# Other charges in the planner that merges TensorE's threads, in a float32 kernel of three transformer layers

## The chip, the core and the metric

The kernel runs on one core of a Trainium2 chip. The metric is the device time of one execution in microseconds, as the median over runs. The profile shows five engines and their queues: TensorE (PE, with its weight loads as PEld), VectorE (DVE), ScalarE (ACT), GpSimd (POOL) and SyncE (SP), which issues the loads of the weights.

## What is computed

A sequence of 256 tokens with 1024 features, with 16 meta tokens ahead of it (272 rows, T = 272), goes through two blocks in float32. The first block has a layer with a gated delta rule and a convolutional feed-forward, and a layer with an mLSTM and the same feed-forward. The second block has a gated feed-forward, three branches side by side (spatial gating, latent attention, attention over a memory of 256 rows) that gates merge, and another gated feed-forward. Cut to its core:

```python
hs = hs + rms_norm(gated_deltanet(rms_norm(hs)))   # 16 heads of 128, chunks, triangular solve per chunk
hs = hs + rms_norm(conv_ffn(rms_norm(hs)))         # 1024 -> 2 x 2816 -> 1024, 3-tap convolution
hs = hs + rms_norm(mlstm(rms_norm(hs)))            # 4 heads
hs = hs + rms_norm(conv_ffn(rms_norm(hs)))
x  = x + 0.5 * swiglu(rmsnorm(x))                  # second block
h  = rmsnorm(x); z = h @ w_in
merged = (gate_a * (spatial_gating(z) @ w_a) + gate_b * (mla(z) @ w_b)
          + gate_c * (memory_attention(z, mem) @ w_c))
x  = x + merged @ w_out
x  = x + 0.5 * swiglu(rmsnorm(x))
```

## The kernel before

Every product of the float32 layers is split into a high and a low part, and three passes (high by high, high by low, low by high) are added up in PSUM. A weight tile comes by a DMA from SyncE's queue (`wraw`), ScalarE makes its high part (`wh`), and VectorE or GpSimd the low part (`wl`). `linear_g` runs such a product: for each tile of weights of 256 columns it issues 48 matmuls for two output tiles of 128 rows.

The order on TensorE is neither written out by hand nor left to the framework. The program is written as Python generators ("threads"). One main thread holds the large products. In some stages side threads are added: in the gated delta rule four lanes that invert the triangular matrices (`wy_inverse`, `gdn_core`), two threads that prepare keys and queries (`before`, with `unit_kq` and `gdn_pre`), one that gates the outputs; in the mLSTM one thread per head; in the branches one each for rope, latent norms, spatial gating and attention. A thread yields a list of tiles that its next matmuls need, at times with an extra delay in us. `Threads.run` keeps a clock for TensorE: it resumes the first thread in its list whose tiles are ready by that clock, and the thread that is ready earliest if none is. Side threads stand ahead of the main thread, so that the large products fill in only where no side thread is ready.

When a tile is ready is what the planner works out while the program is being built. `note` sees each instruction that a thread issues. On TensorE it adds a cost to the clock. On another engine it looks for the first gap in that engine's planned time after its inputs are ready (`place`), as long as the instruction's cost: a fixed part plus one per column, from the table `COST`, times a factor `KC`. `ready` adds a lag when a tile is read: `PLAG` from TensorE to another engine and for a PSUM bank to come free, `LAG` between two other engines, `SAME` on one engine. Casts of weights are placed from TensorE's clock on and count as ready.

`first` sets `KC` and the three lags anew ahead of the gated delta rule, after it, and ahead of the branches. The class's own values hold only until the first of these.

Only TensorE's instructions are pinned to the merged order. The queues of the other engines are ordered by the tile framework, which starts from the order in which the program issues them; some stretches on VectorE and ScalarE are in program order by hand. The thread `projections` chooses between the next group of projections and one of the z products by whether the lanes' preparation of two groups before is over in the plan.

Every recorded instruction stands on line 190, in the engine's wrapper, or on line 383, so the rows are told apart by tiles: `ps` is the output of a large product, `yp`, `w`, `zp` and `r2p` are the products of the inverse, `RT` its two matrices, `Y` a copy between them, `kqp` the transposed keys and queries, `kqtok` their scaled copy, `otp` the transposed outputs, `on` the outputs, `rq_a`, `rq_y` and `rq_o` the steps of a Newton chain for a reciprocal square root (11 instructions, `rsqrt_small`), `cy` the steps of the four-tap filter (three on VectorE for each tile), `zth` the first copy of a z product.

Of the kernel before, what the change touches and what calls it, by code (L numbers as in the profile page):

```python
# [96 lines left out]
class Threads:  # L97
# [1 line left out]

    LAG, SAME, PLAG = 0.25, 0.13, 0.6
    KC = 1.0
    COST = {"PE": (0.0, 1 / 2400), "A": (0.06, 0.00085), "V": (0.07, 0.00104), "G": (0.1, 0.0022)}

    def __init__(self):
        self.clk = {"PE": 0.0}
        self.busy = {k: [] for k in self.COST}
        self.rdy, self.read, self.bank = {}, {}, {}
# [24 lines left out]
    def note(self, key, outs, ins, n, ahead=False):  # L134
        a, b = self.COST[key]
        t = max([self.ready(x, key) for x in ins], default=0.0)
        if key == "PE":
            t = self.clk["PE"] = max(t, self.clk["PE"]) + a + b * n
        else:
            t = self.place(key, self.clk["PE"] if ahead else t, (a + b * n) * self.KC)  # L140
        for x in ins:
            self.read[x.tensor.name] = max(t, self.read.get(x.tensor.name, 0.0))
        for o in outs:
            self.rdy[o.tensor.name] = (0.0, key) if ahead else (t, key)
# [64 lines left out]
class Kern:  # L209
# [1496 lines left out]
    def first(self):  # L1706

        i = self.i
        X = self.embed()
        self.th.KC, self.th.LAG, self.th.SAME, self.th.PLAG = 0.8, 0.25, 0.18, 0.65  # L1710
        Y = yield from self.gdn(X)
        self.th.KC, self.th.LAG, self.th.SAME, self.th.PLAG = 0.9, 0.25, 0.13, 0.6
        self.ordered = True
        self.gctx.close()
        self.pb = self.pool(self.ctx, "pb", 1, space=PSUM)
        self.pp = self.pool(self.ctx, "pp", 3, space=PSUM)
        self.p_v = self.pool(self.ctx, "pkv", 8)
        self.p_m = self.pool(self.ctx, "pm", 1)
        self.p_s2 = self.pool(self.ctx, "psm2", 2)
        b1 = ExitStack()  # L1720
        self.p_b1 = self.pool(b1, "pb1", 1)
        self.p_c = self.pool(b1, "pcore", 12)
        self.lane = None
        vectors = self.vectors_b()
        self.th.add([self.sumsq(self.half, vectors)])
        self.mix_begin(self.hs, T)
        yield from self.project_out(i["gdn_w_out"][0], Y, 16, T, lambda m, p: self.mix_tile(m, p, 8, T))
        X = yield from self.mix_end(self.hs, 16, T, self.ffn_loads(i["ffn_w_up"][0]))
        Y = yield from self.conv_ffn(X, 0, T, 0)
        self.mix_begin(self.hs, T)  # L1730
        yield from self.project_out(i["ffn_w_down"][0], Y, KF, T, lambda m, p: self.mix_tile(m, p, 24, T))
        W = i["ml_w_in"][0]
        X = yield from self.mix_end(self.hs, 32, T, [
            (W, 0, KD, 3072, 8, lambda name, dt: self.cst((128, KD, 8), dt, name, f"m{name}")),
            (W, 0, 4, 0, 256), (W, 0, 4, 512, 256), (W, 4, 4, 0, 256)])
        self.ordered = False
        self.mixing = False
        Y = yield from self.mlstm(X, S + 2)
        self.ordered = True
        self.th.add([self.mem_rows()])  # L1740
        N = S + 2
        hs = [h[:, T - N:] for h in self.hs]
        self.mix_begin(hs, N)

        def then():
            yield from self.ml_heads
            self.mem_load(0, 1)

        yield from self.project_out(i["ml_w_out"][0], Y, 8, N, lambda m, p: self.mix_tile(m, p, 40, N), then)
        self.pause[0].set()  # L1750
        X = yield from self.mix_end(hs, 48, N, self.ffn_loads(i["ffn_w_up"][1]))
        Y = yield from self.conv_ffn(X, 1, N, 2)
        hs = [h[:, NM:] for h in self.hs]
        self.mix_begin(hs, S)
        yield from self.project_out(i["ffn_w_down"][1], Y, KF, S, lambda m, p: self.mix_tile(m, p, 56, S))
        self.pause[1].set()
        X = yield from self.mix_end(hs, PV_F1, S, self.ffn_loads(i["ffn1_w_gu_2"][0]), full=False)
        self.x2 = hs

        def extra(c):  # L1760
            if c == 1:
                self.rope_tables()
                self.th.add([self.mem_keys()])
                self.mem_load(4, 5)
            elif c == 4:
                yield from self.mem_product(4, 5)
            elif c == 7:
                self.mem_load(6, 7)
            elif c == 9:
                yield from self.mem_product(6, 7)  # L1770
                self.mem_done.set()

        Y = yield from self.swiglu_up(X, i["ffn1_w_gu_2"][0], extra, True)
        self.add_begin(PV_MIX)
        yield from self.project_out(i["ffn1_w_down_2"][0], Y, KF, S, lambda m, p: self.add_tile(m, p, 0.5))
        X = self.nextX
        yield self.mem_done
        b1.close()
        self.p_c = None
        self.p_b2 = self.pool(self.ctx, "pb2", 1)  # L1780
        self.th.KC, self.th.LAG, self.th.SAME, self.th.PLAG = 0.9, 0.3, 0.13, 0.7
        yield from self.mixers(X)
        yield from self.last()

# [663 lines left out]
```

## Time and profile before

| | before |
|---|---|
| median of 3 runs | 1668.43 us (1667.3 to 1671.02) |
| the profiled execution | 1671.11 us, span of its instructions 1669.3 us |
| TensorE / VectorE / ScalarE / GpSimd busy | 94% / 67% / 56% / 35% |
| mean granted clock of TensorE | 0.973 |

The span is the time from the first to the last recorded instruction. Busy shares are means over stages with different limits, so each stage is read by itself. In all views times are us unless marked ns; a wait names the instruction that waited and, behind the arrow, the one whose end released it.

### The profile page before, as it was taken

How to read it: one execution, taken by the hardware profiler on the slowest of the kernel's cores; microseconds unless marked ns; L12 is line 12 of the kernel's file. 1: busy time of each engine (PE TensorE's matmuls, PEld its weight loads, DVE VectorE, ACT ScalarE, POOL GpSimd, SP SyncE). 2: the span in 40 equal slices, each digit the busy share in tenths (PEclk: the TensorE clock that was granted, in tenths of full speed). 3: DMA queues.
4: the chain of work that ended last, by engine and by line, in shares of the span. 5: the costliest groups of instructions: out<-in, count | busy, mean ns of one | idle time of the engine just before them, and what ended most of it. 6: DMA issues, size and time to landing. Idle time of an engine off the chain costs nothing.

```text
span 1669.3 us, 31255 instructions
## 1 busy us (share of the span) xinstructions
PE 1564.4 (94%) x11980; PEld 1475.4 (88%) x11980; DVE 1120.0 (67%) x2223; ACT 927.9 (56%) x1877; POOL 579.2 (35%) x535
## 2 busy tenths in 40 slices
PE   8889888899999998999899998999997899999999
PEld 6788778799899997888899998999985789999987
DVE  5788877766888757457877668464659663566643
ACT  4567767655566554446566556454553655564542
POOL 3574555320200002550344441122275548511221
PEclk9799999999999999999999999999998999999999
DMA  5331221226355554335366564566553335656564
GB/s 158 89 89 52 69 64 47 77 90 214 106 178 174 169 175 111 96 115 164 107 185 192 175 185 148 163 199 192 173 166 111 111 93 150 183 164 188 180 189 151
DMA packets 239100, 235.39 MB, mean 141 GB/s; under 512 B 11511, under 2 KB 226407, under 8 KB 238951
## 3 DMA queue, kind: packets, MB, share of 16 engines
q1 hardware_dynamic: 238326, 231.86, 46.4%
q8 instruction: 94, 1.54, 0.4%
q0 software_dynamic: 496, 1.41, 0.4%
q14 instruction: 56, 0.45, 0.1%
q10 hardware_dynamic: 128, 0.13, 0.0%
HBM read 232.32 MB, written 1.05 MB: 140 GB/s over the span
## 4 chain that ended last, share of the span: by engine, by line
PE 68%; DVE 22%; ACT 5%; DMA 3%; issue 2%; POOL 0%; ACTq 0%; POOLq 0%; DVEq 0%
PE ps L190 52%; PE pst L190 5%; DVE cy L190 3%; DVE rq_a L190 3%; ACT wh L190 2%; DVE RT L190 2%; DVE wl L190 1%; DVE rq_y L190 1%; PE memp L190 1%; DMA wraw<-in_ffn_w_up_dram 1%; DVE xn L190 1%; PE rsp L190 1%; DVE on L190 1%; PE w L190 1%; PE up L190 1%
## 5 line engine op out<-in xcount | busy, mean ns | idle before, releaser
L190 PE MATMUL ps<-xhl,wh 128*128 128x256 f32 (+2 forms) x4496 | 861.6, 294 | 28.9 <-DVE py L190 11.1
L190 PEld LDWEIGHTS ps<-xhl,wh 128*128 128x128 f32 x4496 | 703.0, 193 | 38.3 <-DVE py L190 6.9
L190 ACT CAST wh<-wraw 128x1024 fp32r<-128x1024 f32 (+2 forms) x436 | 448.0, 1029 | 389.8 <-PE ps L190 255.9
L190 PE MATMUL ps<-xhl,wl 128*128 128x256 f32 (+2 forms) x2248 | 626.0, 287 | 0.8 <-DVE wl L190 0.8
L383 POOL TENSOR_TENSOR wl<-wraw,wh 128x512 fp32r<-128x512 f32 (+3 forms) x264 | 334.7, 1291 | 658.2 <-ACT wh L190 622.8
L190 PEld LDWEIGHTS ps<-xhl,wl 128*128 128x128 f32 x2248 | 423.9, 192 | 1.0 <-DVE wl L190 1.0
L190 DVE TENSOR_TENSOR wl<-wraw,wh 128x1024 fp32r<-128x1024 f32 (+2 forms) x237 | 287.4, 1213 | 182.4 <-ACT wh L190 179.2
L190 POOL TENSOR_TENSOR wl<-wraw,wh 128x512 fp32r<-128x512 f32 x134 | 173.9, 1319 | 153.1 <-ACT wh L190 136.2
L190 PE MATMUL ps<-hh,wh 128*128 128x256 f32 (+1 forms) x1056 | 191.1, 283 | 0.0
L190 PEld LDWEIGHTS ps<-hh,wh 128*128 128x128 f32 x1056 | 163.2, 189 | 0.0
L190 PE MATMUL ps<-hh,wl 128*128 128x256 f32 (+1 forms) x528 | 149.7, 284 | 0.0
L190 DVE SCALAR_TENSOR_TENSOR fy<-ps,pvt,fy 128x256 f32<-128x256 f32 (+2 forms) x176 | 84.9, 488 | 25.1 <-ACT fy L190 23.2
L190 PEld LDWEIGHTS ps<-hh,wl 128*128 128x128 f32 x528 | 99.4, 188 | 0.0
L190 DVE SCALAR_TENSOR_TENSOR cy<-cx,pvt,cy 128x271 f32<-128x271 f32 (+2 forms) x96 | 74.5, 779 | 13.5 <-ACT cy L190 12.5
L190 DVE TENSOR_TENSOR hh<-fy,hh 128x256 fp32r<-128x256 f32 (+1 forms) x88 | 64.4, 735 | 13.2 <-ACT hh L190 12.8
L190 POOL MEMSET mvt<- 128x4 f32 x4 | 0.4, 102 | 176.0 <-PE ps L190 176.0
L190 ACT ACTIVATE fy<-ps,pvt 128x272 f32<-128x272 f32 (+1 forms) x88 | 49.5, 568 | 12.3 <-PE ps L190 11.8
L190 DVE TENSOR_TENSOR py<-ps,rstd 128x256 f32<-128x256 f32 x72 | 29.9, 420 | 37.9 <-PE ps L190 37.9
L190 PE MATMUL pst<-wh,hh 128*128 128x512 f32 x176 | 55.1, 394 | 0.0
L190 ACT CAST hh<-fy 128x256 fp32r<-128x256 f32 (+1 forms) x88 | 35.7, 407 | 29.8 <-DVE fy L190 29.0
L190 DVE CAST_PREDICATED RT<-lvl,w 128x512 f16<-128x512 uint8 x67 | 44.9, 683 | 7.1 <-PE w L190 6.8
L190 PE MATMUL ps<-og,wh 128*128 128x272 f32 x256 | 48.6, 289 | 0.1
(523 smaller groups left out, 2420.4 us busy)
## 6 DMA issues: line engine op xcount, KB each, us to landing
wraw<-in_ffn_w_up_dram SPq DMA_DIRECT2D x88, 512.0 KB
wraw<-in_ffn_w_gu_dram SPq DMA_DIRECT2D x88, 512.0 KB
wraw<-in_ffn_w_down_dram SPq DMA_DIRECT2D x79, 512.0 KB
wraw<-in_gdn_w_in_dram SPq DMA_DIRECT2D x48, 512.0 KB
wraw<-in_w_in_dram SPq DMA_DIRECT2D x41, 512.0 KB
wraw<-in_ml_w_in_dram SPq DMA_DIRECT2D x24, 512.0 KB
wraw<-in_gdn_w_out_dram SPq DMA_DIRECT2D x16, 512.0 KB
wraw<-in_ml_w_out_dram SPq DMA_DIRECT2D x8, 512.0 KB
```

Of the source, the lines that this page charges most:

```text
L190: r = f(*args, **kw)
L383: eng.tensor_tensor(l[:, a, b], r[:, a, b], h[:, a, b].bitcast(F32), ALU.subtract)
```

## The change

The table of charges gets other numbers: a fixed part for TensorE, larger fixed parts for ScalarE and VectorE, a larger one per column for GpSimd and TensorE. The factor `KC` goes, and so do the three places where `first` sets it and the lags. One set of lags is left for all stages; `SAME` is 0.05.

```diff
-    LAG, SAME, PLAG = 0.25, 0.13, 0.6
-    KC = 1.0
-    COST = {"PE": (0.0, 1 / 2400), "A": (0.06, 0.00085), "V": (0.07, 0.00104), "G": (0.1, 0.0022)}
+    LAG, SAME, PLAG = 0.25, 0.05, 0.6
+    COST = {"PE": (0.006, 0.000441), "A": (0.19, 0.00084), "V": (0.155, 0.00104), "G": (0.1, 0.0025)}
...
         if key == "PE":
             t = self.clk["PE"] = max(t, self.clk["PE"]) + a + b * n
         else:
-            t = self.place(key, self.clk["PE"] if ahead else t, (a + b * n) * self.KC)
+            t = self.place(key, self.clk["PE"] if ahead else t, a + b * n)
...
         X = self.embed()
-        self.th.KC, self.th.LAG, self.th.SAME, self.th.PLAG = 0.8, 0.25, 0.18, 0.65
         Y = yield from self.gdn(X)
-        self.th.KC, self.th.LAG, self.th.SAME, self.th.PLAG = 0.9, 0.25, 0.13, 0.6
         self.ordered = True
...
         self.p_b2 = self.pool(self.ctx, "pb2", 1)
-        self.th.KC, self.th.LAG, self.th.SAME, self.th.PLAG = 0.9, 0.3, 0.13, 0.7
         yield from self.mixers(X)
```

## Rows read from the trace of the kernel before

**Rows 1.** The page: span, and busy us (share of the span) of each engine

```profile
span 1669.3 us, 31255 instructions
...
PE 1564.4 (94%) x11980; PEld 1475.4 (88%) x11980; DVE 1120.0 (67%) x2223; ACT 927.9 (56%) x1877; POOL 579.2 (35%) x535
```

**Rows 2.** Windows: stretch, length, busy us of each engine (instructions), granted clock, DMA

```profile
core 0: us, PE busy (x) PEld busy (x) DVE busy (x) ACT busy (x) POOL busy (x), PEclk, DMA share, GB/s
50.00:350.00 300.00, 260.04 (x2175) 236.84 (x2175) 242.43 (x571) 201.83 (x620) 167.77 (x185) 0.95 0.25 71
640.00:800.00 160.00, 147.08 (x1041) 130.45 (x1039) 100.03 (x245) 81.45 (x178) 55.01 (x46) 0.98 0.39 113
1210.00:1400.00 190.00, 170.01 (x1208) 155.32 (x1207) 125.44 (x359) 99.53 (x214) 109.01 (x89) 0.96 0.42 121
550.00:600.00 50.00, 50.00 (x401) 50.00 (x401) 31.17 (x45) 25.61 (x39) 0.00 (x0) 1.00 0.55 170
```

**Rows 3.** TensorE's waits, 50 to 350 us: total us, times, longest us

```profile
PE yp L190 <- DVE RT L190: 13.7, 10, 3.3
PE kqp L190 <- ACT kqtok L190: 6.7, 4, 3.5
PE otp L190 <- DVE on L190: 5.0, 3, 4.4
PE zp L190 <- DVE RT L190: 4.8, 5, 2.2
```

**Rows 4.** TensorE's waits, 1210 to 1400 us

```profile
PE ps L190 <- DVE py L190: 6.3, 1, 6.3
PE sgy L190 <- DVE sgyy L190: 4.0, 1, 4.0
PE ptp L190 <- ACT pexp L190: 2.9, 1, 2.9
```

**Rows 5.** TensorE's longest wait, 640 to 800 us

```profile
PE mbp L190 <- DVE mlf L190: 4.3, 1, 4.3
```

**Rows 6.** VectorE's groups by shape, 50 to 350 us: busy us, mean ns, idle before

```profile
L190 DVE CAST_PREDICATED RT<-lvl,w 128x512 f16<-128x512 uint8 x67 | 44.9, 683 | 7.1 <-PE w L190 6.8
...
L190 DVE TENSOR_TENSOR rq_a<-rq_a,rq_v 128x4 f32<-128x4 f32 x24 | 8.0, 344 | 0.3
...
L190 DVE MEMSET mga<- 128x24 f32 x1 | 0.1, 78 | 0.0
```

**Rows 7.** ScalarE's groups by shape, 50 to 350 us

```profile
L190 ACT CAST wh<-wraw 128x1024 fp32r<-128x1024 f32 x41 | 43.0, 1049 | 8.2 <-POOL wl L190 3.9 <-issue 2.1 <-PE ps L190 1.1
...
L190 ACT ACTIVATE tcb<-tcb 128x2 f32<-128x2 f32 x1 | 0.2, 197 | 0.0
```

**Rows 8.** One tile over the whole run: duration ns min/median/max, first and last start

```profile
L190 DVE TENSOR_TENSOR rq_a<-rq_a,rq_v x99: 143/161/1277, 9.4 to 1351.8; 128x4 f32<-128x4 f32 x57, 128x3 f32<-128x3 f32 x15, 128x8 f32<-128x8 f32 x15, 128x2 f32<-128x2 f32 x6
```

**Rows 9.** Timelines of VectorE and GpSimd, 194.7 to 198 us: start, us, what

```profile
194.80 0.16 DVE L190 SCALAR_TENSOR_TENSOR rq_a<-rq_y 128x4 f32<-128x4 f32 x1
...
195.34 1.21 DVE L190 TENSOR_TENSOR rq_a<-rq_a,rq_v 128x4 f32<-128x4 f32 x1
196.58 1.19 DVE L190 SCALAR_TENSOR_TENSOR rq_y<-rq_a,rq_y 128x4 f32<-128x4 f32 x1
...
195.25 2.50 POOL L190 TENSOR_TENSOR wl<-wraw,wh 128x512 fp32r<-128x512 f32 x2 [0.66 <-ACT wh L190]
```

**Rows 10.** Windows of the products' tile alone (its PE column is their busy time)

```profile
330.00:340.00 10.00, 6.55 (x44) 5.76 (x44) 0.86 (x2) 0.79 (x2) 1.00 0.19 52
340.00:350.00 10.00, 7.29 (x47) 6.20 (x45) 0.43 (x1) 0.79 (x2) 0.91 0.36 108
```

**Rows 11.** The z products' first copies: ns min/median/max, first and last start

```profile
L190 ACT ACTIVATE zth<-ps x16: 372/397/431, 266.5 to 372.5; 128x272 f32<-128x272 f32 x16
```

## The prediction, made before the changed kernel ran

> **What bounds the kernel now.** I read the totals first, then TensorE's waits, then the engines that it waits for. TensorE is busy for 94% of the span [rows 1]; between the stages that mix threads its products run back to back, 401 matmuls of 272 columns in 50 us, 0.125 us each, with no idle time [rows 2]. Nothing there can move, since one thread alone issues. The change can act where the merge has several threads to choose from: the gated delta rule (50 to 350 us), the mLSTM (640 to 800) and the branches (1210 to 1400). TensorE's idle time there is 40.0, 12.9 and 20.0 us [rows 2], 73 us in all, and that is the pool from which any gain comes. What a reader should see in the waits [rows 3 to 5]: TensorE stands at a lane's instruction, put into its order too early, while VectorE or ScalarE still makes its operand. In the first stage the lanes' inverse (yp and zp, waiting for RT) takes 18.5 us in 15 waits; the transposes behind a Newton chain (kqp and otp) take 11.7 us in 7. In that stage VectorE is busy for 242 of 300 us [rows 2]: close to a bound of its own, so not all of the 40 us can be won.
>
> **The change, part by part.** Nothing is added to or taken from the chip's work. The constants are used while the program is built; the same matmuls, copies and DMAs are issued, in another order on TensorE. The queues of the other engines and SP's loads follow the program's order, so they move with it. Instruction costs are therefore zero on each engine, and the sum consists of waits alone.
>
> What the merge compares is a delay with a number of products put ahead of it, so I convert both sets into products of 272 columns. A product is charged 272/2400 = 0.1133 us before and 0.006 + 272 x 0.000441 = 0.1260 us after; the chip takes 0.125 us [rows 2]. So every delay counts in units that are 11% larger.
>
> *A hop without a queue.* From a matmul through one RT merge (512 columns on VectorE) back to TensorE: before 0.65 + 0.8 x (0.07 + 512 x 0.00104) + 0.25 = 1.382 us, 12.2 products; after 0.6 + 0.155 + 0.532 + 0.25 = 1.537 us, 12.2 products. Through one ScalarE copy of 256 columns: before 0.65 + 0.8 x (0.06 + 0.218) + 0.25 = 1.122 us, 9.9 products; after 0.6 + 0.19 + 0.215 + 0.25 = 1.255 us, 10.0 products. No difference: the shorter lags cancel the longer instructions. So the change does nothing to a lane that meets no queue.
>
> *The queue.* Here the sets differ. VectorE's 49 groups in this stage hold 571 instructions with 109,864 columns (the first and the last of them, and one between, in [rows 6]). Before they are charged 0.8 x (571 x 0.07 + 109,864 x 0.00104) = 123 us, or 1089 products; after 571 x 0.155 + 114.3 = 203 us, or 1610 products; the engine is busy for 242 us. One RT merge is charged 0.48 us before, 0.69 after, and takes 0.683 [rows 6]. ScalarE's 554 instructions with 149,972 columns, in 32 groups without the 66 reads of an accumulator, which are not charged (first and last in [rows 7]), go from 129 to 231 us, against 202 busy [rows 2]. So the plan after sees a queue on VectorE where the plan before saw an engine half idle, and sends a lane's matmul later, with products in front of it.
>
> How much later? Four lanes do the inverse side by side, so up to three RT merges stand in front of one: each is charged 0.69 against 0.48/0.9 = 0.54 in the same units, 0.15 us more, 0.46 for three. Three filter steps (271 columns) in front instead: 0.437 against 0.313, 0.37 for three. I take 0.4 us a wait, in the middle. Fifteen waits x 0.4 = 6.0 us gained, of 18.5 [rows 3]. The bounds: nothing, if the products put ahead were needed later to cover another wait; the whole 18.5 us at most.
>
> *Newton chains.* Eleven tiny VectorE instructions, each after the one before: before 0.18 + 0.8 x 0.074 = 0.239 us each, 23.2 products for the chain; after 0.05 + 0.159 = 0.209 us, 18.3 products. So, without a queue, kqp and otp come 4.9 products, 0.62 us, too early. With a queue at 0.4 us per wait the two nearly cancel: I take zero for the 7 waits (11.7 us now), bounds -2.8 and +8.1 us (13 such chains, 9 before kqp and 4 before otp, x 0.62).
>
> *The other two stages.* In the mLSTM a hop of 256 columns on VectorE is 0.6 + 0.9 x 0.336 + 0.25 = 1.153 us, 10.8 products of 256 (0.1067), and after 1.271 us, 10.7 (0.1189): nothing; its longest wait, 4.3 us, is a chain of tiny instructions with no products beside it that the merge sets [rows 5]. In the branches the lags were longer: 0.7 + 0.303 + 0.3 = 1.303 us, 12.2 products, against 10.7. There the plan after sends lanes 1.5 products, 0.18 us, earlier. The 6.3 us wait for py is a PSUM buffer that products wait for, which no thread's readiness shows [rows 4]; it stays. The other waits are few; I charge +1 us, bounds -4 and +4.
>
> Sum: -6 + 0 + 1 = -5 us. The profiled execution took 1671.1 us (span 1669.3, 1.8 around it), so 1666.1; it lies 2.7 above the median of the runs, 1668.4, and for a run like the median I forecast 1663 us, 0.3% less.
>
> **A rule that speaks against the charges.** The four-element instruction behind "rq_a" takes 143 ns at the least, 161 in the median and 1277 at the most [rows 8]. The timeline shows one such at 0.16 us, and then two at 1.21 and 1.19 us while GpSimd runs two subtractions of 512 columns [rows 9]. The Trainium skill, page SBUF — State Buffer, section "SBUF: two separate sides", says that VectorE with two SBUF inputs (or in a two-port mode) and GpSimd take their common port pair as an exclusive lock for a whole instruction. The trace agrees: the held instruction lasts about as long as GpSimd's. By that rule no fixed part plus columns gives VectorE's time, in either set, and the gain would be near nothing.
>
> **Rivals.** *No change to be told* (within 0.2%, 3.3 us, which is about what a measurement of this kernel tells from no change): TensorE waits because VectorE was held by GpSimd, not because a charge was short. For it: a held instruction costs 1.0 us more than its charge, more than the 0.4 that the change adds to a queue; and VectorE's busy 242 us stay above the 203 charged. Against it: RT itself takes 0.683 on average and is charged exactly that. Result 1665 to 1672.
>
> *Slower by the chains.* A mechanism of its own: the lag between two instructions of one engine falls from 0.18 to 0.05 us, and with it goes a slack that covered the held instructions. It decides if the queue adds less than 0.62 us to a Newton chain in the plan. For it: the means of rq_a are 344 ns [rows 6] against 209 charged. Price: up to 13 x 0.62 = 8 us, and no gain at RT: 1676.
>
> *Slower by an early end of the products.* ScalarE is charged 231 us where it is busy for 202, so the plan's lanes fall behind the chip's, and products run ahead. The last z products cover the lanes' end: 6.6 + 7.3 us of products between 330 and 350 us [rows 10]. If they are used up before, the lanes' last hops stand bare: +10 to +14 us, 1680. The first z tile comes at 266 us today, after all projections [rows 11]; the projections' thread puts a z product in front of a projection whenever the lanes' preparation is late in the plan, which is where this would begin. Against it: 8 z products of 48 matmuls are a long reserve.
>
> *Much faster.* If the orders fit so well that half of the stage's 40 us goes: 1648.
>
> **How the numbers follow.** The forecast's mechanism, more products ahead of lanes that queue at VectorE: 0.45, 0.10 of it the large gain. No difference to be told: 0.25. Slower by the chains: 0.17. Slower by early products: 0.13. Faster 0.45, same 0.25, slower 0.30. The time is that of the likeliest, 1663; its own range is 1652 to 1665. The range takes in the other cases down to the large gain and up to the early end, 1649 to 1679, and leaves out their tails, about 2 in 10.
>
> **What would show it.** Right: the same instruction counts; the waits of yp and zp for RT in the first stage fall from 18.5 us to about 12, TensorE's idle time there from 40 to about 34 us, and VectorE's busy time stays near 242. The chains: kqp and otp above 11.7 us. The early end: z tiles before 266 us, or TensorE idle between 330 and 360. Wrong altogether: the first stage as long as before with its idle time only moved, or a difference that comes from a stage with one thread, by another order of loads or of GpSimd's share.

## The result, and the profile after

The changed kernel takes 1717.28 us (median of four runs, 1715.38 to 1717.59); the kernel before, measured beside it, 1667.87 us. The ratio is 1.0284, with a 95% interval of 1.0265 to 1.0303: slower by 2.8%, where 0.3% faster was forecast. The page of the changed kernel, its totals and the clock that TensorE was granted in 40 equal slices:

```profile
span 1715.6 us, 31253 instructions
PE 1587.4 (93%) x11980; PEld 1495.2 (87%) x11980; DVE 1116.1 (65%) x2223; ACT 931.1 (54%) x1877; POOL 579.8 (34%) x535
PEclk9899989987999999999999999999999999999999
```

Every engine issues as many instructions as before [rows 1], and VectorE, ScalarE and GpSimd are busy as long within 4 us: only the order changed. But the clock's digits show an 8 and a 7 in the ninth and tenth slice, 343 to 429 us, where the page of the kernel before has nines. So I cut the run where stages hand over, at the first matmul of a product that opens the next one, and for `mm` at its last (us):

| from, to | before | after | more |
|---|---|---|---|
| start, the gated delta rule's output product (`og`) | 368.3 | 403.0 | 34.7 |
| `og`, the mLSTM's gates (`psmg`) | 275.6 | 279.1 | 3.5 |
| `psmg`, the branches' first product (`krp`) | 572.3 | 575.8 | 3.5 |
| `krp`, the branches' last product (`mm`) | 258.6 | 263.0 | 4.4 |
| `mm`, end | 194.5 | 194.7 | 0.2 |

Three quarters of the 46.3 us are lost in the first stage that mixes threads. Windows of that stage, cut at 300 us and at its end, for the kernel before (columns as in [rows 2]):

```profile
50.00:300.00 250.00, 215.78 (x1791) 195.74 (x1790) 204.85 (x470) 171.59 (x532) 145.37 (x166) 0.94 0.25 71
300.00:368.30 68.30, 61.88 (x524) 58.05 (x523) 42.91 (x117) 40.15 (x110) 24.93 (x21) 0.98 0.26 78
```

and after:

```profile
50.00:300.00 250.00, 218.75 (x1760) 204.29 (x1759) 181.68 (x391) 159.75 (x450) 161.37 (x173) 0.92 0.32 91
300.00:403.00 103.00, 72.24 (x539) 59.93 (x538) 64.04 (x201) 56.15 (x191) 7.28 (x14) 0.83 0.04 11
```

Length minus TensorE's busy time is its idle time. Up to 300 us it is 31.3 us after against 34.2 before, 3 us better. From there to the end it is 30.8 against 6.4, 24.4 us worse, and the same work takes longer: TensorE is busy for 291.0 us over both windows against 277.7, 13.3 more, at a granted clock of 0.83 in the last window where it was 0.98. These three, -3.0 + 24.4 + 13.3, are the 34.7 us. The 13.3 us are not the clock's alone: one matmul of the product `og` lasts 288 ns in the median, but back to back one follows every 125 ns [rows 2], so a matmul that stands alone counts for more busy time than one in a row; no run separates the two. The other columns say what is missing at the end: VectorE did 391 instructions up to 300 us where it had done 470, and the DMA share of the last window is 0.04 where it was 0.26: there are no weights left to load, so no products left to run.

TensorE's waits after, 50 to 400 us, so that the longer stage is taken in whole (total, times, longest):

```profile
PE yp L189 <- DVE RT L189: 13.6, 9, 3.8
PE ps L189 <- ACT cy L189: 8.9, 6, 5.2
PE ps L189 <- DVE zs L189: 8.7, 4, 6.4
PE kqp L189 <- ACT kqtok L189: 6.3, 4, 2.1
PE otp L189 <- DVE on L189: 4.6, 3, 2.2
...
PE zp L189 <- DVE RT L189: 0.8, 2, 0.5
```

In the same window the rows of the kernel before are those of [rows 3], and its products wait for their buffers for 3.8 us:

```profile
PE ps L190 <- DVE zs L190: 2.6, 3, 1.9
...
PE ps L190 <- ACT cy L190: 1.2, 2, 1.0
```

The inverse waits 14.4 us for RT against 18.5, the Newton chains 10.9 us against 11.7. (Up to 350 us alone, the window of [rows 3], it is 12.3 and 7.0 us, but by then the changed kernel has not done as much of the stage.) The waits that the change could shorten did get shorter, by 4.9 us; against that, products wait 17.6 us for the buffers that VectorE (`zs`) and ScalarE (`cy`) read out, 13.8 more. What else it paid shows where products are. The z products' first copies (ns at least, in the median, at most; first and last start):

```profile
L189 ACT ACTIVATE zth<-ps x16: 391/401/478, 116.3 to 305.2; 128x272 f32<-128x272 f32 x16
```

The first comes at 116 us, not at 266, and the last at 305 instead of 372 [rows 11]. The windows of the products' tile alone (`ps`), from the start until the fourth lane has finished its inverse, before:

```profile
0.00:151.84 151.84, 79.29 (x463) 67.49 (x463) 0.00 (x0) 14.00 (x36) 0.89 0.35 100
```

and after, with three stretches of the stage's end:

```profile
0.00:193.16 193.16, 123.78 (x768) 109.36 (x768) 3.04 (x7) 21.64 (x55) 0.91 0.41 114
...
300.00:310.00 10.00, 3.48 (x21) 2.61 (x20) 0.86 (x2) 0.81 (x2) 0.95 0.32 103
310.00:320.00 10.00, 0.00 (x0) 0.00 (x0) 0.00 (x0) 0.00 (x0) 0.71 0.01 3
...
390.00:400.00 10.00, 0.00 (x0) 0.00 (x0) 0.00 (x0) 0.00 (x0) 0.50 0.00 0
```

The stage has 1152 such matmuls. After, 768 of them have run when the first four lanes are through, before 463. The 305 more take 38 us at 0.125 us each [rows 2], and the first group is 41.3 us late. From then on the four groups of lanes follow each other as before: from the end of the first group's inverses to that of the fourth 180.0 us against 177.5. What is left of the stage then takes 29.8 us against 39.0; together 41.3 + 2.6 - 9.2 = 34.7 us. The last product has run at 310 us, 93 us before the stage ends, where before products filled the stretch up to its end [rows 10]. In that bare stretch the granted clock goes up and down: 1.00 from 320 to 340 us, 0.83 from 340 to 370, and 0.50, the lower of its two levels, 1.2 GHz, from 390 to 400. One kind of matmul of the lanes' last steps, before:

```profile
L190 PE MATMUL up<-wq,St x32: 195/276/276, 352.9 to 356.2; 128*128 128x32 f32 x32
```

and after:

```profile
L189 PE MATMUL up<-wq,St x32: 261/401/401, 387.7 to 394.2; 128*128 128x32 f32 x32
```

276 ns became 401. The Trainium skill, page TensorE: Matmul & The Clock Gate, section "Part 1: The HAM clock gate", has a half-rate state that activity lifts; the trace agrees, with the granted 0.50 and the 401 ns above, and with 1.00 from 410 to 420 us, when products run back to back again.

### The profile page after: what moved, and what is told of

It reads as the page before. It is cut to its first block, busy times and chain, and to the rows that moved or that the text cites. A ratio compares the mean times of both kernels' runs of the same rounds, so it can differ in the third digit from the quotient of the medians.

```text
span 1715.6 us, 31253 instructions
## 1 busy us (share of the span) xinstructions
PE 1587.4 (93%) x11980; PEld 1495.2 (87%) x11980; DVE 1116.1 (65%) x2223; ACT 931.1 (54%) x1877; POOL 579.8 (34%) x535
## 4 chain that ended last, share of the span: by engine, by line
PE 72%; DVE 17%; ACT 6%; DMA 2%; issue 2%; POOL 1%; ACTq 0%; POOLq 0%; DVEq 0%
PE ps L189 55%; PE pst L189 4%; DVE cy L189 2%; DVE rq_a L189 2%; ACT wh L189 2%; DVE RT L189 1%; PE memp L189 1%; DVE rq_y L189 1%; DVE wl L189 1%; PE warm L189 1%; PE up L189 1%; PE rsp L189 1%; PE w L189 1%; DVE xhl L189 1%; PE dp L189 1%
## 5 line engine op out<-in xcount | busy, mean ns | idle before, releaser
L189 PE MATMUL ps<-xhl,wh 128*128 128x256 f32 (+2 forms) x4496 | 864.2, 295 | 44.3 <-DVE py L189 10.6
L189 PEld LDWEIGHTS ps<-xhl,wh 128*128 128x128 f32 x4496 | 710.7, 194 | 54.9 <-ACT cy L189 10.5
L189 PEld LDWEIGHTS ps<-xhl,wl 128*128 128x128 f32 x2248 | 428.2, 194 | 0.9 <-DVE wl L189 0.9
L189 DVE SCALAR_TENSOR_TENSOR cy<-cx,pvt,cy 128x271 f32<-128x271 f32 (+2 forms) x96 | 74.8, 783 | 14.3 <-ACT cy L189 11.7
L189 DVE TENSOR_TENSOR hh<-fy,hh 128x256 fp32r<-128x256 f32 (+1 forms) x88 | 60.6, 691 | 13.4 <-ACT hh L189 13.2
L189 ACT ACTIVATE fy<-ps,pvt 128x272 f32<-128x272 f32 (+1 forms) x88 | 49.6, 569 | 13.8 <-PE ps L189 13.2
L189 DVE CAST_PREDICATED RT<-lvl,w 128x512 f16<-128x512 uint8 x67 | 45.1, 683 | 11.7 <-PE w L189 11.3
```

The lines of the kernel that those rows point to most:

```text
L189: r = f(*args, **kw)
```

## The experiments

The theory after the result: larger charges put the lanes' instructions later in the plan, products go ahead of the first group's chain, and they are missing at the end. Its rivals: the loss is in the other stages; it comes from the one place where z products are chosen; from GpSimd, which held the products' copies; or the lanes simply meet longer waits. A last question was whether an order between the two does better. This table is worked out from the windows of each run like those above: ratio to the kernel before, products run until the fourth lane's inverse and the time of that, end of the stage, TensorE's idle time from 50 to 300 us and from 300 us to the stage's end.

| kernel | ratio | products | 4th lane, us | stage's end, us | idle to 300 | idle after 300 |
|---|---|---|---|---|---|---|
| before | 1 | 463 | 151.8 | 368.3 | 34.2 | 6.4 |
| e11 tie order | 1.0052 | 464 | 153.9 | 374.4 | 37.1 | 6.1 |
| e1 old set in the stage | 1.0148 | 464 | 154.0 | 379.1 | 35.7 | 12.2 |
| f1 new lags only | 1.0152 | 447 | 151.2 | 386.3 | 42.5 | 12.5 |
| e5 charges x 0.6 | 1.0220 | 414 | 141.6 | 393.5 | 45.8 | 17.2 |
| e12 PSUM seen | 1.0169 | 450 | 154.1 | 391.8 | 44.2 | 14.0 |
| g2 longer lag | 1.0174 | 483 | 153.0 | 391.2 | 39.8 | 14.6 |
| f3 dearer products | 1.0138 | 493 | 153.6 | 382.2 | 39.7 | 11.1 |
| e3 old ScalarE charge | 1.0196 | 525 | 162.6 | 389.3 | 37.0 | 16.2 |
| f2 shorter occupancy | 1.0213 | 549 | 168.8 | 395.1 | 37.7 | 17.7 |
| e6 charges x 0.8 | 1.0179 | 552 | 167.0 | 383.2 | 43.7 | 12.9 |
| g1 x 0.8, old lags | 1.0189 | 561 | 165.0 | 385.7 | 33.6 | 17.2 |
| e4 z last | 1.0242 | 576 | 168.9 | 392.4 | 34.0 | 20.9 |
| e7 old VectorE charge | 1.0396 | 694 | 198.0 | 422.2 | 42.8 | 28.8 |
| e8 no GpSimd filter | 1.0217 | 729 | 173.7 | 391.1 | 27.9 | 27.5 |
| e2 new set in the stage | 1.0242 | 741 | 197.7 | 405.0 | 33.5 | 26.9 |
| after | 1.0284 | 768 | 193.2 | 403.0 | 31.3 | 30.8 |

e9 and e10 (below) leave this stage as it was before. Their profiles end it at 365.2 and 364.2 us, with 34.0 and 37.9 us idle up to 300 us and 6.3 and 6.4 behind it, so a difference of about 4 us between two rows tells nothing. Diffs that set the table or the lags for this stage set them back behind it; a short diff shows the changed part of the table or of the lags only.

**Which stage.** The kernel before with the new set in the gated delta rule alone, and the changed kernel with the old one there:

```diff
-        self.th.KC, self.th.LAG, self.th.SAME, self.th.PLAG = 0.8, 0.25, 0.18, 0.65
...
+        self.th.COST, (self.th.LAG, self.th.SAME, self.th.PLAG) = {"PE": (0.006, 0.000441), "A": (0.19, 0.00084), "V": (0.155, 0.00104), "G": (0.1, 0.0025)}, (0.25, 0.05, 0.6)
         Y = yield from self.gdn(X)
...
```

> The kernel before with the new charges and lags in the gated delta rule alone. Theory 1: 1702 to 1710 us, z tiles among the projections, no large products at all from about 310 us to the stage's end. Rival (all mixed stages alike): 1680 to 1690 us.

```diff
+        self.th.COST, (self.th.LAG, self.th.SAME, self.th.PLAG) = {"PE": (0.0, 1 / 2400), "A": (0.048, 0.00068), "V": (0.056, 0.000832), "G": (0.08, 0.00176)}, (0.25, 0.18, 0.65)
         Y = yield from self.gdn(X)
...
```

> The changed kernel with the old charges and lags put back in the gated delta rule alone. Theory 1 (products run ahead of the lanes in that stage and leave its end bare): the stage is back at its old length, the output product starts near 368 us and not at 403, the time is 1674 to 1682 us, with what is left (about 6 us in the mLSTM, 4 in the branches) from the two later stages. Rival (the loss comes from all mixed stages about alike): 1695 to 1705 us.

The first took 1710.90 us, ratio 1.0242 [1.0227, 1.0258], its stage ending at 405.0: the loss is there with nothing else changed (0.9 us above what was expected of it). It also hands something on: from `og` to `psmg`, where one thread issues, it takes 279.1 us, as in the changed kernel, against 275.6. In the changed kernel TensorE waits 3.3 us there for `og`, and the clock is granted 0.95 over the first 50 us against 1.00 before. The second took 1692.33, 1.0148 [1.0123, 1.0173]. Its first group is back (464 products, 154.0 us), but the stage ends at 379.1: of 34.7 us, 23.9 came back. 10.8 stayed, though charges and lags are those of before. This lies between the two expectations, and e11 (below) was made to tell why.

The new set in the mLSTM alone, and from the branches to the end alone, both in the kernel before:

```diff
+        self.th.COST, self.th.KC, (self.th.LAG, self.th.SAME, self.th.PLAG) = {"PE": (0.006, 0.000441), "A": (0.19, 0.00084), "V": (0.155, 0.00104), "G": (0.1, 0.0025)}, 1.0, (0.25, 0.05, 0.6)
         Y = yield from self.mlstm(X, S + 2)
...
```

> The kernel before with the new charges and lags in the mLSTM alone; the gated delta rule keeps its order. Theory (the later stages lose by the new set on their own, apart from the first): from the first gate matmul to the last transpose 122 to 125 us instead of 118, 1672 to 1676 us. Rival (the 6 us seen there in the changed kernel come from what the first stage hands on): within 2 us of the kernel before.

```diff
-        self.th.KC, self.th.LAG, self.th.SAME, self.th.PLAG = 0.9, 0.3, 0.13, 0.7
...
+        self.th.COST, self.th.KC, (self.th.LAG, self.th.SAME, self.th.PLAG) = {"PE": (0.006, 0.000441), "A": (0.19, 0.00084), "V": (0.155, 0.00104), "G": (0.1, 0.0025)}, 1.0, (0.25, 0.05, 0.6)
         yield from self.mixers(X)
```

> The kernel before with the new charges and lags from the branches to the end. Theory: the branches take 261 to 263 us instead of 259, 1671 to 1675 us. Rival (handed on): within 2 us of the kernel before.

In the mLSTM: 1669.32 us, 1.0006 [0.9995, 1.0017], no difference. One tile each of the stage's start, of its end and of the branches' start, in the kernel before:

```profile
L190 PE MATMUL psmg<-xhl,wh x16: 282/287/488, 643.9 to 654.0; 128*8 128x272 f32 x16
...
L190 PE MATMUL mtp<-eye,mwd x8: 208/218/231, 737.6 to 761.7; 16*128 16x16 f32 x8
...
L190 PE MATMUL krp<-xhl,wh x16: 278/280/468, 1216.2 to 1219.6; 128*32 128x256 f32 x16
```

and with the new set in the mLSTM:

```profile
L190 PE MATMUL psmg<-xhl,wh x16: 283/287/488, 640.7 to 650.8; 128*8 128x272 f32 x16
...
L190 PE MATMUL mtp<-eye,mwd x8: 208/219/232, 738.9 to 763.9; 16*128 16x16 f32 x8
...
L190 PE MATMUL krp<-xhl,wh x16: 277/280/468, 1213.1 to 1216.5; 128*32 128x256 f32 x16
```

From `psmg` to the last `mtp` it takes 123.2 us against 117.8, but 572.4 against 572.3 until `krp`: the 5.4 us are given back by the products that follow. In the branches, 1673.78 us, 1.0027 [1.0016, 1.0039]: the stage grows from 258.6 to 264.7 us, a small loss that stays, in a time as expected. The mLSTM's run went as its rival had it: the 3.5 us that the changed kernel loses from `psmg` to `krp` do not come from the new set there alone, and no run shows from what.

**What in the stage.** Four edits of the changed kernel. First, z products only when no projection is left:

```diff
-                elif nz < 6 or not todo:
+                elif not todo:
```

> The changed kernel with all charges new, but the projections' thread never takes a z product while a group of projections is still to come: it waits for the lanes' preparation. The lanes' places in the plan stay late. Theory 1c (what costs is that z products are spent early, so that nothing covers the end): z tiles from about 250 us on to the end, at least two thirds of the loss back, 1680 to 1692 us. Rival 1d (what costs is each lane's lateness in the order, wherever the z products stand): the lanes end as late as in the changed kernel, 1705 to 1720 us.

1710.66 us, 1.0242 [1.0225, 1.026]. The first z copy moves from 116 to 239 us, yet only 10.6 of the 34.7 us come back, though the first group ends 24.2 us earlier; the time is the rival's. 576 products still stand in front of the first group, projections now: the early z products are the sign of the loss more than its cause. Second, the filter steps that GpSimd took go to VectorE:

```diff
-        if ct >= 14:
+        if ct >= 99:
```

> The changed kernel with the last two steps of the four-tap filter taken from GpSimd and given to VectorE as one instruction, for 18 tiles. Theory 2 (products that run ahead pile up behind GpSimd, which makes their low parts at about 2.6 us a tile: where it lags, PSUM's two buffers are not freed and TensorE stands): GpSimd is 29 us less busy, TensorE's waits of ps for cy and zs between 50 and 210 us fall from 15 to under 6 us, 1700 to 1709 us. Rival (the lanes' lateness alone, and VectorE gets 10 us more work): 1714 to 1725 us.

1704.67 us, 1.0217 [1.02, 1.0234]. TensorE's waits of products for a buffer, 50 to 210 us, in the changed kernel:

```profile
PE ps L189 <- DVE zs L189: 8.0, 3, 6.4
PE ps L189 <- ACT cy L189: 7.1, 5, 5.2
```

and with the filter off GpSimd:

```profile
PE ps L189 <- ACT cy L189: 4.0, 6, 1.6
PE ps L189 <- DVE zs L189: 3.6, 3, 1.9
```

15.1 us became 7.6, and the first group ends 19.4 us earlier, with nearly as many products in front of it (729). From 50 us to that point the clock is granted 1.00 here, 0.92 in the changed kernel. So 19.4 of the first group's 41.3 us go with GpSimd's share and the buffers that waited for it, 4.9 of them as 39 products fewer, and the number of products alone does not make the 41.3; the time is the theory's, though the waits stay above the 6 us that it gave. The bare end stays, 27.5 us idle. The other two give one engine its old charge in this stage:

```diff
-"A": (0.19, 0.00084)
+"A": (0.048, 0.00068)
```

> The changed kernel, in the gated delta rule with ScalarE's old charge (0.048 us + 0.00068 per column, the old one with its factor 0.8) and all else new. Theory 1a (ScalarE's charge is what makes the plan's lanes late): no z tile ahead of a projection, some z tiles left after 300 us, three quarters of the stage's loss back, 1682 to 1692 us. Rival 1b (VectorE's charge, or the shorter lag on one engine, does it): under a third back, above 1702 us.

```diff
-"V": (0.155, 0.00104)
+"V": (0.056, 0.000832)
```

> The changed kernel with VectorE's old charge (0.056 us + 0.000832 per column) in the gated delta rule and all else new, ScalarE's too. Theory 1a (ScalarE's charge makes the plan's lanes late, VectorE's little): under a third of the loss back, 1702 to 1714 us. Rival 1b (VectorE's charge matters as much): 1702 us or less.

ScalarE's: 1701.81 us, 1.0196 [1.0178, 1.0214], 525 products, 13.7 of the stage's 34.7 us back: between the theory and its rival. Of the 305 products too many in front of the first group, 243 go with ScalarE's charge. VectorE's: 1734.36 us, 1.0396 [1.038, 1.0411], slower than either set whole, which neither side had expected. Its windows:

```profile
50.00:300.00 250.00, 207.24 (x1650) 192.42 (x1651) 180.10 (x365) 154.18 (x442) 157.49 (x167) 0.91 0.29 83
300.00:422.20 122.20, 93.38 (x660) 78.74 (x658) 75.56 (x227) 63.09 (x202) 16.02 (x20) 0.75 0.09 30
```

It idles on both sides, 42.8 us up to 300 and 28.8 behind it. With 694 products in front of the first group, a short VectorE charge beside ScalarE's new one takes only 74 of them back, and yp's waits for RT, 21.0 us in 50 to 400 us, are longer than the 13.6 of the changed kernel.

**The level.** If too many products go ahead, smaller charges should find an order with as few as before and short waits. All three engines' charges times 0.6 and times 0.8 in this stage, and times 0.8 with the old lags:

```diff
-"A": (0.19, 0.00084), "V": (0.155, 0.00104), "G": (0.1, 0.0025)
+"A": (0.114, 0.000504), "V": (0.093, 0.000624), "G": (0.06, 0.0015)
```

> The changed kernel with all its charges for ScalarE, VectorE and GpSimd in the gated delta rule times 0.6; the new lags and TensorE's new charge stay. Theory 1 (what decides is the level of the charges, which sets how many products stand in front of each hop of a lane): the first group's lanes end near 165 us as in the kernel before, the output product starts at 368 to 380 us, 1675 to 1692 us. Rival (the shorter lags let the lanes come too early and TensorE stands at Newton chains): waits of kqp and otp above 20 us in the stage, 1700 us or more.

```diff
+"A": (0.1520, 0.000672), "V": (0.1240, 0.000832), "G": (0.0800, 0.002000)
```

> The same with the factor 0.8, the old factor on the new charges. Theory 1: between the changed kernel and the run with 0.6: first group's lanes end between 170 and 200 us, 1688 to 1704 us. Rival (no order between level and time, the merge's orders scatter): outside of that.

```diff
-(0.25, 0.05, 0.6)
+(0.25, 0.18, 0.65)
```

> The changed kernel, in the gated delta rule with its charges times 0.8 and the old lags (0.18 on one engine, 0.65 from TensorE). Theory (too high a level of the charges and too short a lag are two causes): waits of kqp and otp fall from 23.5 us with the new lags and 0.8 to under 15, 1678 to 1690 us. Rival (longer lags only put the lanes later still): more products before the first group's inverses end than the 552 with the new lags, and 1695 us or more.

At 0.8: 1697.79 us, 1.0179 [1.0162, 1.0196], 552 products. At 0.6: 1705.32 us, 1.022 [1.0205, 1.0235], although only 414 products go ahead and the first group ends 10 us earlier than in the kernel before. Its windows and its waits, 50 to 400 us:

```profile
50.00:300.00 250.00, 204.17 (x1693) 187.15 (x1692) 195.75 (x458) 165.69 (x515) 141.53 (x162) 0.92 0.23 68
300.00:393.50 93.50, 76.34 (x618) 71.83 (x615) 57.64 (x137) 50.82 (x133) 31.78 (x26) 0.93 0.23 68
...
PE yp L189 <- DVE RT L189: 27.3, 19, 3.1
PE kqp L189 <- ACT kqtok L189: 17.9, 4, 7.1
```

Here TensorE stands at the lanes again: RT 27.3 us, and with otp's 3.9 the Newton chains 21.8, where the changed kernel has 10.9 for the chains in the same window. So the smaller charges lose 25 us of the stage and the larger ones 35, for opposite reasons. The 0.6 run went as its rival had it; the theory's "near 165 us as in the kernel before" misread that kernel, where the group ends at 151.8. The time at 0.8 lies in its range, but not between 0.6 and the changed kernel, as the theory had it: the level does not order the times. With the old lags at 0.8: 1699.38 us, 1.0189 [1.0167, 1.0212], no better, as the rival had it: 561 products, and the chains wait 17.7 us instead of 23.5.

**One part alone.** The kernel before with the new lags in this stage only:

```diff
-        self.th.KC, self.th.LAG, self.th.SAME, self.th.PLAG = 0.8, 0.25, 0.18, 0.65
+        self.th.KC, self.th.LAG, self.th.SAME, self.th.PLAG = 0.8, 0.25, 0.05, 0.6
```

> The kernel before with the new lags (0.05 on one engine, 0.6 from TensorE) in the gated delta rule; all charges old. Theory (the charges did it, the lags not): some 430 to 470 products before the first group's inverses end, 463 before; the time within the scatter of orders, 1667 to 1682 us. Rival (the lags lose by themselves, lanes too early at Newton chains): waits of kqp and otp above 20 us, 1685 us or more.

1693.07 us, 1.0152 [1.0127, 1.0177]. Its waits, 50 to 400 us:

```profile
PE kqp L190 <- ACT kqtok L190: 15.8, 5, 6.8
PE yp L190 <- DVE RT L190: 14.9, 13, 3.6
...
PE otp L190 <- DVE on L190: 6.8, 3, 4.4
```

This went as the rival had it. The chains wait 22.6 us against 11.7: a price of the slack that goes with the lag of 0.18. In the changed kernel, with the same lags and the larger charges, it is 10.9. The opposite, a longer lag in the kernel before:

```diff
-        self.th.KC, self.th.LAG, self.th.SAME, self.th.PLAG = 0.8, 0.25, 0.18, 0.65
+        self.th.KC, self.th.LAG, self.th.SAME, self.th.PLAG = 0.8, 0.25, 0.25, 0.65
```

> The kernel before with the lag on one engine in the gated delta rule 0.25 instead of 0.18; a try at a faster version. Theory (the lag is the slack that covers VectorE's held instructions in the Newton chains): waits of kqp and otp under 10 us, 1655 to 1668 us. Rival (orders of this level scatter, and the one before is a fortunate one): 1672 to 1690 us.

1698.29 us, 1.0174 [1.0144, 1.0204]. The chains' waits fall to 7.2 us as meant, but RT's rise to 20.3, and 14.6 us stand idle at the end: slower than the theory and the rival had it. The changed kernel with a queue charge that is shorter than the time until a result is ready:

```diff
-            t = self.place(key, self.clk["PE"] if ahead else t, a + b * n)
+            d = self.OVER.get(key, 0.0)
+            t = self.place(key, self.clk["PE"] if ahead else t, a + b * n - d) + d
...
+        self.th.OVER = {"A": 0.1, "V": 0.06, "G": 0.03}
```

> The changed kernel where in the gated delta rule a planned instruction blocks its engine for 0.1 us (ScalarE), 0.06 (VectorE) or 0.03 us (GpSimd) less than its charge, while its result is ready as late as before. Theory (the new charges are durations, and the plan's engines fill up because they are taken for occupancy): 500 to 580 products before the first group's inverses end, 1685 to 1700 us. Rival (the long delay of each hop does it, not the fill of the engines): above 700 products, 1705 us or more.

1703.02 us, 1.0213 [1.0184, 1.0241]: 549 products, as the queue's part of the theory has it, in a time that lies between the theory's and the rival's. And with a dearer product, so that fewer fit into a delay:

```diff
-"PE": (0.006, 0.000441)
+"PE": (0.0075, 0.000551)
```

> The changed kernel with TensorE's charge in the gated delta rule times 1.25, which is far more than a product takes on the chip; all other charges and the lags stay new. Theory (only the ratio of a lane's delay to a product's charge decides how many products stand ahead): as with 0.8 on the other charges, 500 to 570 products before the first group's inverses end, 1688 to 1702 us. Rival (a charge further from the chip's makes the order worse): 1710 us or more.

1689.88 us, 1.0138 [1.0112, 1.0164], 493 products: the unit alone brings the stage's end from 403.0 to 382.2. Of the orders of the changed kernel this is the best by a little, and still 1.4% slower than before.

**How much of it is chance, and two tries at a better order.** One lag of the kernel before by 0.01 us, which is 0.11 us over the eleven instructions of a Newton chain, less than one product, and swaps what nearly ties:

```diff
-        self.th.KC, self.th.LAG, self.th.SAME, self.th.PLAG = 0.8, 0.25, 0.18, 0.65
+        self.th.KC, self.th.LAG, self.th.SAME, self.th.PLAG = 0.8, 0.25, 0.17, 0.65
```

> The kernel before with the lag on one engine in the gated delta rule 0.17 instead of 0.18, which means nothing for the chip and gives another order at ties. Theory (the level of the charges decides, and orders of one level scatter by some us): within 4 us of the kernel before, either way. Rival (the order before is a fortunate one of its level, as the 10.8 us in that stage with the old charges put back would have it): 1675 to 1685 us.

1677.35 us, 1.0052 [1.0033, 1.0071]: 8 us, more than the change was forecast to bring, and what the rival had. So two orders of the same level differ by 0.5%, and e1's remaining 10.8 us are of that size. The second try, after g2, lets a product's thread wait for its PSUM bank in the plan:

```diff
...
+        if ps is None and not self.ordered and not self.mixing and self.gdn_stage:
+            yield ["pp"]
         ps = ps or [self.ps((128, N)) for _ in range(nm)]
+        self.th.bank["pp"] = ps[-1].tensor.name
...
```

> The kernel before, where in the gated delta rule a large product also waits in the plan for its PSUM buffers to be free, so that lanes are put ahead of a product that could not start. A try at a faster version. Theory 2 (products in the order too early, while PSUM is not free, hold up the lanes): faster by 3 to 12 us, 1656 to 1665 us. Rival (in the kernel before products hardly wait for PSUM, 3.8 us in that stage): within 4 us of it or slower by the scatter of orders.

1695.85 us, 1.0169 [1.014, 1.0198]: yp's waits for RT rise to 30.4 us, as with the small charges. No order that was tried beats the kernel before.

## Why the prediction was wrong

**What bounds the kernel**: right in the main. The stage that was named first has three quarters of the lost time, and the instruction counts stayed. "Nothing there can move", of the stretches with one thread, fails by the 3.5 us behind `og`. VectorE's "close to a bound of its own" was not put to the test: its busy time, 245.7 us after and 247.8 before, lies in a stage that got 34.7 us longer.

**A hop without a queue**: the number of products in a hop is the same in both sets, as worked out, but f3 shows how much hangs on that number: 25% on the product's charge took 275 products out of the front of the first group.

**The queue** is the step that failed. "Sends a lane's matmul later, with products in front of it" happened, and part of its gain came: 18.5 us of waits for RT fell to 14.4 over the stage, 4.1 of the 6.0 us forecast. But TensorE's idle time in the stage did not fall from 40 to 34 us; it rose from 40.6 to 62.0. The step counted only what a product covers and took the product itself as free. A product in front of a matmul of the first group's lanes that covers no wait moves the group's end by its 0.125 us: 305 more are 38 us of work, and the group ended 41.3 us later. The two numbers agree by chance in part, since in e8 729 products stand there and the group is 21.9 us late; the rest hung on the buffers that products waited for, and on the clock. All 1152 products are needed once, so what goes ahead is missing at the end. And the engine was the wrong one: the step put the queue at VectorE, but without ScalarE's new charge 525 of the 768 products are left in front (e3), without VectorE's 694 (e7). The bound that was given, "nothing, if the products put ahead were needed later", stopped at zero; the runs put it at 34.7 us of loss, of which 23.9 come back with the old set (e1) and 10.8 stay with it.

**Newton chains**: forecast zero; the waits went from 11.7 to 10.9 us over the stage, inside the bounds. The balance that was assumed is there: f1, with the lags and without the charges, has 22.6 us.

**The other two stages**: the mLSTM nothing, measured nothing (e9). The branches +1, bounds 4 either way; measured 4.5 us as a ratio, with an interval of 2.7 to 6.5, and 6.1 in the stage (e10), at the upper bound or past it.

**The rule against the charges**: VectorE is still held by GpSimd as before (below), and it did not bring "no change". What it is worth no run separates: e8, which takes 27 us of work off GpSimd, shortens the stage by 11.9 us, and its shorter waits for buffers are seen, but not whether VectorE's held instructions had a part in them.

**The rivals.** "Slower by an early end of the products" was the right mechanism, and both its signs came: a first z tile before 266 us, and TensorE idle behind 330 us. It got a chance of 0.13 and a price of 10 to 14 us; it came at 34.7. Its argument against, "8 z products of 48 matmuls are a long reserve", weighed the reserve by itself, not against ScalarE's larger charge, which the same rival named and which e3 shows to put most of the products ahead. And the price held only the cover that is lost, 14 us: the idle time at the end grew by 24.4, and 13.3 us more of busy time, part of it at the lower clock, were left out. "Slower by the chains" is what the milder sets do (e5, f1), not this change.

What stays open: why VectorE's old charge beside ScalarE's new one is worse than both sets whole, and why the order before beats others with as many products ahead of the first group by 6 to 18 us (e11, e1, f1). The table says that it idles less than f1 up to 300 us, and less than e1 and f1 behind it; which placing does it was not found. Nor does the number of products ahead set the stage's end by itself: 450 (e12) and 729 (e8) end it at 391.8 and 391.1 us, for other waits.

## What to carry to other kernels

When several threads are merged into one in-order queue, filler work had two prices here: what it does not cover lies on the chain in front of which it stands, and it is missing later, when the last chains run bare and the clock falls. So read the idle time at the stage's end together with the idle time within it, and count how much filler has run when the first chain is through. Charges that are closer to the real durations need not make a better order: this planner's numbers worked as one setting, so change one and count again; and measure how far two equivalent orders lie apart (here 0.5%, in e11) before believing in a gain below that. Let the window of a wait reach to the stage's end in both kernels: cut at 350 us, the longer stage looked better than it was.

## What the runs showed of the hardware

GpSimd stopped the three other engines, one behind the other. The timeline of the changed kernel, 110 to 118 us (start, duration, engine, what, and in brackets the idle time before):

```profile
113.06 2.48 POOL L189 TENSOR_TENSOR wl<-wraw,wh 128x512 fp32r<-128x512 f32 x2
...
115.50 0.75 POOL L189 TENSOR_TENSOR kv<-cth,cy 128x272 f32<-128x272 f32 x1
...
116.28 0.40 ACT L189 ACTIVATE zth<-ps 128x272 f32<-128x272 f32 x1 [2.73 <-POOL kv L189]
116.71 0.44 DVE L189 SCALAR_TENSOR_TENSOR zs<-zth,ps 128x272 f32<-128x272 f32 x1 [5.13 <-ACT zth L189]
...
117.20 0.82 PE L189 MATMUL ps<-xhl,wh 128*128 128x272 f32 x2 [6.35 <-DVE zs L189]
```

One filter step on GpSimd stands behind two subtractions of 512 columns; ScalarE's copy waits for it, VectorE's step for the copy, and TensorE for the buffer, 6.35 us: three hops, none longer than 0.8 us of work. A tiny instruction of VectorE, over the whole run:

```profile
L189 DVE TENSOR_TENSOR rq_a<-rq_a,rq_v x99: 132/161/1300, 9.3 to 1400.0; 128x4 f32<-128x4 f32 x57, 128x3 f32<-128x3 f32 x15, 128x8 f32<-128x8 f32 x15, 128x2 f32<-128x2 f32 x6
```

161 ns in the median and 1300 at the most, as before [rows 8]: by the Trainium skill, page SBUF — State Buffer, section "SBUF: two separate sides", VectorE with two inputs in SBUF and GpSimd hold their common ports as a lock for a whole instruction, and the trace agrees: the longest, at 1359.76 us, runs beside three subtractions on GpSimd that start at 1357.28 and take 3.76 us, about 1.25 each. And the clock fell to its lower level, 0.50, in a stretch where TensorE is still busy for most of the time: 8.66 us of the ten from 390 to 400 us in the second row below, with 34 matmuls of the lanes and no product. In the ten before it was busy for 6.78 us, at 0.70; from 320 to 330 us, for 7.90 us at 1.00.

```profile
380.00:390.00 10.00, 6.78 (x36) 5.71 (x35) 5.77 (x25) 1.82 (x8) 0.00 (x0) 0.70 0.01 2
390.00:400.00 10.00, 8.66 (x34) 6.70 (x34) 2.19 (x3) 4.45 (x9) 0.00 (x0) 0.50 0.00 0
```
